# A hybrid encoder layer on one core: order of differences, tables, masks and late tiles up to attention, and splits, scales and places in the joints behind it

## The chip, the cores and the metric

The kernel is one program on one core of one Trainium2 chip. A core has engines that run side by side, each with its own queue of instructions that it works off in order: TensorE (PE) multiplies matrices into the accumulator memory PSUM, VectorE (DVE) does elementwise arithmetic, ScalarE (ACT) does activations, copies and casts, GpSimd (POOL) does odd elementwise work and issues transfers, SyncE (SP) only issues transfers. The metric is device microseconds (us) of one execution. The profile was taken on one execution of its own, and every row below is from it.

## The reference

One layer over 1024 tokens of width 1024, in float32. Three sub-layers follow each other, each between two RMS norms:

```python
h = swiglu(rmsnorm(x, ffn1_pre_g), ffn1_w_gate, ffn1_w_up, ffn1_w_down)   # 1024 -> 2816 -> 1024
x = x + 0.5 * rmsnorm(h, ffn1_post_g)
h = rmsnorm(x, mix_pre_g)
q, k, v = split(h @ w_qkv)                        # 16 heads of 64
o_na  = neighbourhood_attention(q[:8], k[:8], v[:8], na_rel_bias)      # 16 x 64 grid, window 8 x 16
o_dil = dilated_mixture_attention(q[8:], k[8:], v[8:], t5_rel_bias)    # windows (128,1), (512,4), (2048,16)
x = x + rmsnorm(concat(rmsnorm(o_na), rmsnorm(o_dil)) @ w_out, mix_post_g)
h = swiglu(rmsnorm(x, ffn2_pre_g), ffn2_w_gate, ffn2_w_up, ffn2_w_down)
x = x + 0.5 * rmsnorm(h, ffn2_post_g)
```

The matrix products of the two feed-forward layers, of q and k, of v and of the output projection carry nearly all of the work.

## The kernel before, in words

**Precision.** A float32 product is made of three faster ones (`mm3`, lines 317 to 319): each operand is split into a rounded part `hi` (a cast, on ACT, L413 or L673) and the rest `lo` (a subtraction, on DVE, L414 or L674), and hi*hi, hi*lo and lo*hi are summed in PSUM.

**Seven products for eight.** Each large product is cut into 2 x 2 blocks and done with seven block products on sums and differences of blocks (S1 to S4 on the left, T1 to T4 on the right). The tokens are 8 tiles of 128; tiles 0 to 3 are the upper half, 4 to 7 the lower. For a lower tile, the sums need the upper tile's block back: `early_half` loads it into a tile `x1` (a transfer issued by POOL, L212), and `right_half` makes the sums on DVE (L276 to L279, L272) and splits them (L268, L269).

**`PairGemm`** does gate and up (22 pairs) and q and k (8 pairs). The first `early` pairs run a part of their work `ahead` (the blocks A11 and A12, for which the lower tiles aren't needed yet), while the lower tiles are still being normed, transposed and summed. Then `run` goes over all pairs b; for an early pair it issues the products S2, the last product of the pair before (`last`), S1, S3 and S4 (12 matmuls each, `last` 12 too), 60 matmuls in all; a later pair does A11, `last`, S2, A12, S1, S3 and S4, 84 matmuls. Meanwhile it prepares the weights of pair b + 1: `direct` is three subtractions (L502 to L504) on weights just loaded, `second`, `sums` and `rest` are splits. On DVE there lie besides: u2 (L540), v (L548), c22 (L567), c21 (L575), and for q and k the `put` of each result: scale, cast (ACT, L925 to L930), subtraction (DVE, L931), and transfers to DRAM (POOL, L936 to L942). PE may begin S4 only when v has read the accumulator that S4 goes on with.

**`Passes`** does the down projections and v: seven passes over chunks, each chunk loaded (`praw`), cast (L673), subtracted (L674).

**The stages**, by the trace: first feed-forward layer with its early pairs, pair loop and seven down passes up to 690 us; early v passes and early q/k pairs to 768; the other v passes to 828; the pair loop of q and k to 946; attention (dilated heads, then neighbourhood heads) to 1184; output projection to 1265; second feed-forward layer, as the first, to the end at 1926.

**What sets the order.** PE runs in the order in which the program writes its instructions. For the other engines a planner sets the order, by its own estimates of durations: of the instructions whose inputs it takes to be ready, it puts an earlier written one first, and it may pull a later one ahead where it believes the engine idle. `c.behind(f, E)` takes that freedom away: what f issues on engine E stays behind the last instruction of E written so far. `plan(n, {turn: [...]})` hands out extra steps: one turn after each block of matmuls (`c.tick`). Steps with several parts go through `c.steps` and `c.sums`, from which every six matmuls take one each (`c.step`).

**Names used below.** `F` norms two tiles of the first layer, `A` adds the residual for two tiles and norms them (L788, then L150 on ACT, the small DVE steps L133 to L143, L204), `U` transposes a tile and makes its blocks (PE L157). `value_sums` are the differences of the v weights (`RightSums.sums`, DVE L385 to L387; one buffer `tr`, loaded again when the sums are stored). `masks` are nine steps of mask additions on POOL for the neighbourhood heads. `c.toeplitz` are eight transfers that spread the bias tables in DRAM (POOL, L852). `pg.start` loads the first two weight blocks, `split_left(0)` splits the first. `most` issues squares of the neighbourhood heads' outputs (ACT, L1213), whose norm (L131 to L143, L1220) the output projection needs first. `Finish.half` and `Finish.end` are the end of a layer: square on ACT (L150), product with the gain (DVE, L750), reciprocal root (L128 to L143), addition (L767), store (L768).

## Time and profile before

| | us |
|---|---|
| median of 3 runs | 1929.8 (1928.88 to 1931.73) |
| the profiled execution | 1927.83 |
| its span, first to last instruction | 1926.0 |
| PE busy | 1851.6 (96%) |
| DVE busy | 1325.9 (69%) |
| ACT busy | 832.0 (43%) |
| POOL busy | 319.9 (17%) |

A row of the timeline gives start, duration (both in us), engine, line of the kernel, operation, what it writes <- what it reads, the shape and how many in a row; in brackets the engine's idle time before it and what ended it. A row of the waits gives who waited for what: us in all, how many times, the longest. A row of the windows gives the stretch, its length, then for PE, PE's weight loads, DVE, ACT and POOL the busy us and the count of instructions, then the granted PE clock as a share of full speed, the share of time in which the transfer engines were busy, and GB/s.

### The profile page before, as it was taken

Reading aid. Unit: us, or ns where it says so; the run is one execution under the profiler, and the core shown is the slowest. Engines: PE = TensorE matmul, PEld = TensorE weight load, DVE = VectorE, ACT = ScalarE, POOL = GpSimd, SP = SyncE. Lnnn points to the kernel's source line nnn. Section 1 sums busy time; section 2 is a strip of 40 time slices with the busy share of each in tenths; the row PEclk is TensorE's granted clock in tenths of the full one; section 3 lists DMA queues with packets and bytes.
Section 4 is the critical chain, followed back from the end, with each engine's and each line's share of the span. In section 5 each row is a group of like instructions: output and inputs, shape, how many; then the busy total and the mean of one; then the engine's idle time right before and its main releaser. Section 6 shows DMA issues by size and latency. Waiting matters only on the chain.

```text
span 1926.0 us, 25147 instructions
## 1 busy us (share of the span) xinstructions
PE 1851.6 (96%) x8904; PEld 1536.5 (80%) x8904; DVE 1325.9 (69%) x2233; ACT 832.0 (43%) x1491; POOL 319.9 (17%) x504
## 2 busy tenths in 40 slices
PE   7899999999999989998899998999999999999997
PEld 6787888888778867877799997877888888888886
DVE  6777776765565875556677765777788777654557
ACT  7422333333344555223488765455222333344332
POOL 2123211111030122122433100121111111110000
PEclk9999999999999999999999999999999999999999
DMA  7656565547886757556968540575456655476563
GB/s 270 211 169 207 204 225 211 195 164 248 295 306 216 269 187 257 193 178 221 299 224 259 170 142 23 190 280 186 158 192 238 216 193 210 159 267 216 200 227 136
DMA packets 169296, 404.95 MB, mean 210 GB/s; under 512 B 17793, under 2 KB 40225, under 8 KB 167122
## 3 DMA queue, kind: packets, MB, share of 16 engines
q1 hardware_dynamic: 121330, 242.66, 37.9%
q0 software_dynamic: 46832, 158.59, 22.9%
q10 hardware_dynamic: 1008, 2.10, 0.3%
q8 instruction: 70, 1.15, 0.2%
q14 instruction: 56, 0.46, 0.1%
HBM read 277.34 MB, written 130.99 MB: 212 GB/s over the span
## 4 chain that ended last, share of the span: by engine, by line
PE 47%; issue 27%; DMA 9%; DVE 9%; POOL 3%; ACT 3%; SPq 1%; DVEq 0%; POOLq 0%; ACTq 0%
PE mmp L319 9%; PE mmp L317 9%; PE mmp L318 9%; PE accp L318 4%; PE accp L319 4%; PE accp L317 4%; PE po L1072 2%; PE ptp L982 2%; DMA wraw<-in_wqk_dram 2%; PE po L1184 2%; DMA wraw<-in_wu_dram 1%; DVE pw L674 1%; DMA tsv<-tr 1%; PE sp L1051 1%; DVE wlo L414 1%
## 5 line engine op out<-in xcount | busy, mean ns | idle before, releaser
L317 PE MATMUL mmp<-x,whi 128*128 128x512 f32 (+1 forms) x1464 | 581.4, 397 | 19.4 <-DVE v L548 10.9
L319 PE MATMUL mmp<-x,wlo 128*128 128x512 f32 (+1 forms) x1464 | 577.5, 394 | 3.9 <-DVE wlo L414 3.9
L318 PE MATMUL mmp<-x,whi 128*128 128x512 f32 (+1 forms) x1464 | 575.7, 393 | 1.3 <-DVE x L240 0.8
L317 PEld LDWEIGHTS mmp<-x,whi 128*128 128x128 f32 x1464 | 278.2, 190 | 84.7 <-ACT whi L413 10.0
L319 PEld LDWEIGHTS mmp<-x,wlo 128*128 128x128 f32 x1464 | 277.9, 190 | 68.6 <-DVE wlo L414 5.9
L318 PEld LDWEIGHTS mmp<-x,whi 128*128 128x128 f32 x1464 | 278.3, 190 | 62.6 <-DVE x L240 1.1
L674 DVE TENSOR_TENSOR pw<-praw,pw 128x1024 fp32r<-128x1024 f32 (+1 forms) x181 | 199.7, 1148 | 115.7 <-ACT pw L673 115.3
L673 ACT CAST pw<-praw 128x1024 fp32r<-128x1024 f32 (+1 forms) x181 | 168.6, 982 | 208.3 <-PE accp L319 150.3
L318 PE MATMUL accp<-pw 128*128 128x512 f32 x600 | 234.4, 391 | 5.9 <-DVE pw L674 5.6
L317 PE MATMUL accp<-pw 128*128 128x512 f32 x600 | 234.8, 391 | 0.3 <-DVE hb L730 0.2
L319 PE MATMUL accp<-pw 128*128 128x512 f32 x600 | 233.6, 389 | 0.0
L413 ACT CAST whi<-wraw 128x1024 fp32r<-128x1024 f32 x129 | 135.3, 1051 | 219.1 <-PE mmp L318 184.5
L414 DVE TENSOR_TENSOR wlo<-wraw,whi 128x1024 fp32r<-128x1024 f32 x129 | 158.2, 1228 | 19.9 <-ACT whi L413 19.7
L318 PEld LDWEIGHTS accp<-pw 128*128 128x128 f32 x600 | 112.7, 188 | 31.6 <-DVE pw L674 9.0
L317 PEld LDWEIGHTS accp<-pw 128*128 128x128 f32 x600 | 112.7, 188 | 25.1 <-ACT pw L673 1.2
L319 PEld LDWEIGHTS accp<-pw 128*128 128x128 f32 x600 | 112.6, 188 | 23.3
L621 POOL DMA_DIRECT2D g<-sg x44 | 23.9, 544 | 471.1 <-DVE sg L614 296.4
L413 ACT CAST whi<-traw 128x512 fp32r<-128x512 f32 x52 | 32.4, 623 | 152.3 <-DVE traw L503 95.6
L502 DVE TENSOR_TENSOR wraw<-wraw 128x1024 f32<-128x1024 f32 x52 | 63.7, 1225 | 45.4 <-DMA wraw<-in_wqk_dram 26.2
L432 ACT COPY s<-mmp 128x512 f32<-128x512 f32 x52 | 30.6, 588 | 139.4 <-PE mmp L319 136.4
L575 DVE TENSOR_TENSOR c<-mmp,u 128x512 f32<-128x512 f32 x52 | 35.9, 690 | 76.9 <-PE mmp L319 76.8
L1184 PE MATMUL po<-vs,pt 128*128 128x128 f32 x352 | 50.3, 276 | 2.0 <-ACT pt L984 1.7
(278 smaller groups left out, 2761.1 us busy)
## 6 DMA issues: line engine op xcount, KB each, us to landing
praw<-g SPq DMA_DIRECT2D x70, 512.0 KB, 6.0
wraw<-in_wg_dram SPq DMA_DIRECT2D x44, 512.0 KB, 4.2
wraw<-in_wu_dram SPq DMA_DIRECT2D x44, 512.0 KB, 6.2
tr<-in_wd_dram SPq DMA_DIRECT2D x44, 512.0 KB, 6.5
g<-sg POOLq DMA_DIRECT2D x88, 256.0 KB, 4.1
ts<-tr POOLq DMA_DIRECT2D x22, 1024.0 KB, 4.8
praw<-ts SPq DMA_DIRECT2D x88, 256.0 KB, 4.3
praw<-in_wd_dram SPq DMA_DIRECT2D x66, 256.0 KB, 4.9
```

The lines of the kernel that those rows point to most:

```text
L317: nc.tensor.matmul(out, ahi, bhi, start=start, stop=False, skip_group_check=go_on)
L318: nc.tensor.matmul(out, ahi, blo, start=False, stop=False, skip_group_check=go_on)
L319: nc.tensor.matmul(out, alo, bhi, start=False, stop=stop, skip_group_check=go_on)
L413: nc.scalar.copy(hi, raw)
L414: nc.vector.tensor_sub(lo, raw, hi.bitcast(F32))
L502: nc.vector.tensor_sub(r[:, 0:2], r[:, 1:3], r[:, 0:2])
L575: nc.vector.tensor_add(c21, d, u2)
L673: nc.scalar.copy(hi, raw[:, :m])
L674: nc.vector.tensor_sub(lo, raw[:, :m], hi.bitcast(F32))
L982: nc.tensor.transpose(ps[:, j, :], src[:, j * P:(j + 1) * P], c.ident)
L1072: nc.tensor.matmul(po[:, un * 2 + j], pt[:, 2 * j + t, :], rhs, start=t == 0, stop=t == 1)
L1184: nc.tensor.matmul(po[0][:, u], pt[0][:, j, :], vs[:, k0 + j, :], start=j == 0, stop=j == n - 1)
```

## The change

Nothing is computed otherwise; instructions change place, order, queue or buffer.

- **Differences.** `direct` of the pair loop (three subtractions on DVE) is pinned behind the last DVE instruction written before it.
- **Tiles.** In the first layer, the norm of tiles 6 and 7 is written one turn earlier and both norms are pinned on ACT; the transposes of tiles 6 and 7 come one turn later. For q, k, v the transposes of tiles 4 to 7 come later and the residual of tiles 6, 7 is written at turn 10 instead of 4. In the second layer tiles 6 and 7 come one turn earlier. Outside the first layer the upper half for tiles 5 and 7 is loaded into a buffer of the `x` tiles, as soon as tile 4 or 5 has been transposed, and that of tile 6 when tile 4 is done.
- **Masks and tables.** The mask steps alternate with the differences of the v weights, two to one; the eight table transfers go from the pair loop of q and k to the v passes before it, one every second turn.
- **q and k.** The second half of k is put away right after its sum (`third`) and no longer with the second half of q in `last`; the last pair's q goes to DRAM by SP instead of POOL.
- **Joints.** `most` is called one turn earlier and takes a turn at once. In the second layer the first weights are loaded two turns earlier, and their split is made before the layer begins, into a buffer of its own. In the last layer the product with the gain goes into a tile `hm` of its own for the first half of tiles 4 to 7.

```diff
         self.parts[t] = deque(((A11, xn[:, :T]), (A12, xn[:, T:])))
-        if t >= 4:
+        if t == 4 or t > 4 and c.xn:
             self.early_half(t)
     def early_half(self, t):
         c = self.c
-        x1 = self.half[t] = c.xp.tile([P, 2, 4, P], F32, tag="x1", name="x1", bufs=c.deep)
+        if t % 2 and not c.xn:
+            x1 = c.xp.tile([P, D], F32, tag="x", name="x1", bufs=c.xbufs).rearrange("p (i k x) -> p i k x", i=2, k=4)
+        else:
+            x1 = c.xp.tile([P, 2, 4, P], F32, tag="x1", name="x1", bufs=c.deep)
+        self.half[t] = x1
...
             self.open -= 1
+            if t == 4 and not c.xn:
+                self.early_half(6)
         a22 = transposed(c, src)
+        if t in (4, 5) and not c.xn:
+            self.early_half(2 * t - 3)
...
                 if last:
                     last()
-                direct()
+                c.behind(direct, DVE)
                 second()
...
                 self.sink.first(b, pb, False, s1)
-                direct()
+                c.behind(direct, DVE)
                 second()
...
             nc.vector.tensor_add(c22, d, v)
+            self.sink.third(b, c22)
             sums()
...
         sumsq(self.c, h, self.ss[:, t, g:g + 1])
-        self.c.nc.vector.tensor_mul(h, h, self.gain[:, g * T:(g + 1) * T])
+        to = h
+        if self.last and t >= 4 and g == 0:
+            to = self.part = self.c.xp.tile([P, T], F32, tag="hm", name="hm")
+        self.c.nc.vector.tensor_mul(to, h, self.gain[:, g * T:(g + 1) * T])
...
-            nc.vector.scalar_tensor_tensor(x[:, sl], h[:, sl], r, x[:, sl], op0=ALU.mult, op1=ALU.add)
+            nc.vector.scalar_tensor_tensor(x[:, sl], h[:, sl] if g else self.part, r, x[:, sl], op0=ALU.mult, op1=ALU.add)
...
+    def third(self, b, k):
+        self.put(b, 1, 1, k)
+
     def last(self, b, q, k):
         self.put(b, 0, 1, q)
-        self.put(b, 1, 1, k)
...
-                nc.gpsimd.dma_start(dst, e[:, j].bitcast(F32).rearrange("p (s x) -> p s x", s=8))
+                (nc.sync if h and b == 7 else nc.gpsimd).dma_start(dst, e[:, j].bitcast(F32).rearrange("p (s x) -> p s x", s=8))
...
-            early_pools(e)
+            early_pools(e, 2 if pg.own else 3)
...
-            spread(more + masks, 36)
+            steps = more[:1]
+            for i, f in enumerate(more[1:]):
+                steps += masks[2 * i:2 * i + 2] + [f]
+            spread(steps + masks[2 * len(more[1:]):], 36)
...
-            F = lambda *ts: lambda: op0.norm(ts, [xs[t] for t in ts])
+            F = lambda *ts: lambda: c.behind(lambda: op0.norm(ts, [xs[t] for t in ts]), ACT)
...
-                                    {0: [F(4, 5), L(6, 7)], 1: [U(4)], 2: [F(6, 7), U(5)], 4: [U(6)], 5: [U(7)]},
+                                    {0: [F(4, 5), L(6, 7)], 1: [U(4), F(6, 7)], 2: [U(5)], 5: [U(6)], 6: [U(7)]},
...
-            plan(12, {0: [lambda: fin.scale(4, 4), A(4, 5)], 4: [A(6, 7)], 7: [U(4)], 9: [U(5), lambda: queued(pg.start)],
-                      11: [lambda: pg.split_left(0)]})
+            plan(12, {0: [lambda: fin.scale(4, 4), A(4, 5)], 8: [U(4), lambda: queued(pg.start)],
+                      10: [lambda: pg.split_left(0), A(6, 7)]})
             vp.run(0, 1, upto=1)
...
-            plan(8, {1: [U(6)], 3: [U(7)]})
+            plan(8, {0: [U(5)], 3: [U(6)], 5: [U(7)]})
             pg.ahead()
...
+            plan(20, {2 * i: [f] for i, f in enumerate(c.toeplitz)})
             vp.run(2, 3)
...
-            plan(8, {**{i: c.toeplitz[2 * i:2 * i + 2] for i in range(4)}, 5: [lambda: queued(load_head)], 7: [lambda: queued(load_head), lambda: queued(first_bias),
+            plan(8, {5: [lambda: queued(load_head)], 7: [lambda: queued(load_head), lambda: queued(first_bias),
...
                     c.todo.append(lambda n=n, i=i: c.behind(lambda: n.squares(slice(0, 448), 0, (i, i + 1)), ACT))
+            c.tick()
...
-                        c.todo.extend([lambda: None, most])
+                        c.todo.append(most)
...
+            pg.own = pool("p0", 1, prep, side="right")
...
-            plan(12, {0: [lambda: fin.scale(0, 4), A(0, 1)], 2: [A(2, 3)], 5: [U(0)], 6: [U(1)], 7: [G(4)],
-                      8: [lambda: queued(pg.start), G(5)], 9: [U(2)], 10: [U(3)], 11: [G(6)]})
+            plan(12, {0: [lambda: fin.scale(0, 4), A(0, 1)], 2: [A(2, 3)], 5: [U(0)], 6: [U(1), lambda: queued(pg.start)], 7: [G(4)],
+                      8: [G(5)], 9: [U(2)], 10: [U(3), lambda: pg.split_left(0)], 11: [G(6)]})
...
-                {0: [G(7), lambda: fin.scale(4, 4), A(4, 5)], 1: [A(6, 7)], 3: [U(4)], 4: [U(5)], 6: [U(6)], 7: [U(7)]},
+                {0: [G(7), lambda: fin.scale(4, 4), A(4, 5)], 1: [A(6, 7)], 3: [U(4)], 4: [U(5)], 5: [U(6)], 6: [U(7)]},
```

More of the change, by code (lines that the diff above doesn't have):

```diff
@@ L622, in second, with third @@
         self.got[b, 0] = g
+    def third(self, b, up):
+        pass
     def last(self, b, gate, up):
@@ L739, with __init__ @@
 class Finish:
-    def __init__(self, c, src, dst, gain, op):
-        self.c, self.src, self.dst, self.gain, self.op = c, src, dst, gain, op
+    def __init__(self, c, src, dst, gain, op, last=False):
+        self.c, self.src, self.dst, self.gain, self.op, self.last = c, src, dst, gain, op, last
         self.ss = c.small.tile([P, 8, 2], F32, tag="fss", name="fss", bufs=1)
@@ L1373, in ffn @@
             c.pw, c.pr, c.ha, c.tj = pool("pw", 5, w), pool("pr", 4, w), pool("ha", 1, w), pool("tj", 1, m)
-            fin = Finish(c, src, dst, load_gain(c, post, "post"), None)
+            fin = Finish(c, src, dst, load_gain(c, post, "post"), None, pre is None)
             hs = {}
```

## The prediction

> **What bounds the kernel now.** I read the page first, then the waits of PE, then windows around each of these waits, then the timeline inside them.
>
> ```profile
> PE 1851.6 (96%) x8904; PEld 1536.5 (80%) x8904; DVE 1325.9 (69%) x2233; ACT 832.0 (43%) x1491; POOL 319.9 (17%) x504
> ```
>
> PE is busy for 1851.6 of 1926.0 us, so an edit that leaves its work alone can win at most what PE stands still or runs slowly for. The waits of PE (total, times, longest) say where:
>
> ```profile
> PE mmp L317 <- DVE v L548: 10.9, 7, 2.8
> PE accp L318 <- DVE pw L674: 6.0, 7, 1.7
> PE trp L157 <- DVE x L204: 5.5, 1, 5.5
> PE trp L157 <- DVE xn L204: 4.9, 1, 4.9
> PE gps L304 <- DMA xn<-in_ffn_pre_g_dram: 4.4, 1, 4.4
> PE mmp L317 <- ACT whi L413: 4.4, 2, 2.3
> PE mmp L319 <- DVE wlo L414: 3.9, 3, 3.1
> PE po L1072 <- ACT pt L984: 3.2, 4, 1.0
> PE sp L1051 <- DVE sa L972: 2.9, 1, 2.9
> PE mmp L317 <- ACT x L238: 2.6, 1, 2.6
> PE trp L1231 <- DVE og L1220: 2.5, 1, 2.5
> ```
>
> Of these only L304 (the kernel's start) and L1072 (inside attention) lie where nothing is changed. Windows of the places that the change touches (length, then busy time, granted clock, DMA share, GB/s):
>
> ```profile
> 26.00:35.00 9.00, 5.55 (x19) 4.01 (x18) 5.05 (x16) 4.25 (x9) 3.75 (x7) 0.81 1.02 406
> 40.00:62.00 22.00, 16.47 (x72) 12.94 (x72) 18.66 (x36) 13.65 (x23) 4.09 (x8) 0.92 0.70 234
> 480.00:545.00 65.00, 59.00 (x249) 45.82 (x248) 37.31 (x40) 28.67 (x39) 4.67 (x7) 1.00 0.86 302
> 695.00:728.00 33.00, 24.38 (x100) 19.25 (x99) 26.13 (x52) 19.09 (x33) 10.09 (x18) 0.90 0.63 214
> 775.00:860.00 85.00, 83.45 (x366) 68.16 (x364) 52.10 (x66) 22.78 (x26) 16.75 (x28) 1.00 0.51 167
> 855.00:882.00 27.00, 21.79 (x90) 17.30 (x89) 18.72 (x24) 9.99 (x12) 9.36 (x14) 0.94 0.72 207
> 882.00:945.00 63.00, 57.55 (x251) 46.46 (x250) 39.53 (x53) 19.82 (x28) 15.86 (x22) 1.00 0.82 270
> 945.00:960.00 15.00, 10.31 (x58) 9.42 (x56) 7.66 (x29) 10.26 (x28) 9.15 (x9) 0.77 1.00 340
> 1184.00:1204.00 20.00, 15.61 (x75) 11.72 (x74) 15.20 (x50) 7.78 (x28) 0.60 (x2) 0.91 0.00 1
> 1264.00:1274.00 10.00, 7.50 (x22) 5.32 (x21) 8.70 (x20) 4.46 (x9) 1.63 (x4) 0.66 0.76 263
> 1305.00:1340.00 35.00, 31.37 (x133) 23.96 (x132) 27.56 (x40) 20.13 (x34) 6.48 (x12) 0.95 0.56 189
> 1340.00:1690.00 350.00, 350.00 (x1526) 286.18 (x1525) 261.44 (x331) 105.76 (x140) 46.73 (x82) 1.00 0.56 194
> 1915.00:1926.00 11.00, 0.57 (x3) 0.14 (x1) 6.60 (x21) 0.72 (x2) 0.00 (x0) 0.67 0.26 95
> ```
>
> The pair loop from 1340 to 1690 shows PE full: 350/1526 = 0.229 us a matmul, so a turn of 12 is 2.75 us and one of 24 is 5.5. In the other windows the loss has two parts: the idle time (length less PE's busy time) and the slow clock (length times one less the granted clock).
>
> **The change part by part.** Each place with its loss, what I take of it and, in brackets, both ends.
>
> (1) *Norm of tiles 4 and 5 pinned on ACT.* Loss in 26–35: 3.45 + 9 x 0.19 = 1.7.
>
> ```profile
> 27.64 1.07 ACT L150 ACTIVATE xn<-x 128x1024 f32<-128x1024 f32 x1
> ```
>
> This square was pulled ahead of the cast L238 that PE waits 2.6 for. Pinned, it comes after; but the same norm then ends about two squares (2.1) later, and ACT's queue holds back L413 while a tile is still being loaded. Take 1.5 [-1: the 2.6 gone and two squares and a split of 1.5 in exchange; 4].
>
> (2) *Tiles 6, 7: norm a turn earlier, transposes a turn later.* Loss in 40–62: 5.53 + 1.76.
>
> ```profile
> 56.58 2.48 DVE L204 SCALAR_TENSOR_TENSOR xn<-x,y,gain 128x1024 f32<-128x1024 f32 x2
> ```
>
> PE waits 4.9 for it, with 18.66 of 22 us of DVE taken by sums and splits. The norm starts up to a turn (5.5) earlier and PE asks a turn later: more than the wait. What may be late next is tile 7's splits ahead of the pair loop, now 5.5 nearer to it. Take 6 [3: half the wait and its clock; 7.3].
>
> (3) *Differences of the v weights between the masks.* Loss in 480–545: 6.0, for L674.
>
> ```profile
> 516.00 1.23 DVE L385 TENSOR_TENSOR tr<-tr 128x1024 f32<-128x1024 f32 x1 [7.35 <-DMA tr<-in_wv_dram]
> ```
>
> With one buffer `tr`, each group is stored before the next load; DVE waits in order, and L674 behind it. With two masks between, the steps are six to eight turns apart (16 to 22 us) and the load has landed. What covers it: the transfers, already at 0.86 of their time here, with the mask additions now in the same stretch on POOL, where the stores queue behind them. Take 4.5 [0; 6].
>
> (4) *Residual of tiles 4 to 7 for q, k, v.* Loss in 695–728: 8.62 + 3.3.
>
> ```profile
> 692.42 4.87 DVE L788 SCALAR_TENSOR_TENSOR x<-hb,y,x 128x1024 f32<-128x1024 f32 x4
> ```
>
> Two of these four (1.22 each) and a second reciprocal root leave from ahead of L204, for which PE waits 5.5, and U(4) comes 2.75 later: 2.4 + 2.75 = 5.2 of the 5.5. The other wait, 3.1 for L414, stood behind tile 5's sums, which move to `ahead`; but there the residual and norm of tiles 6, 7 now take DVE for two L788 (2.4), two L204 (2.48 by the row in (2)) and some ten small steps (1.7), 6.6 together, so I count half. With the clock, take 7.5 [3: the wait of 3.1 alone; 11.9].
>
> (5) *`direct` pinned in q and k; tables and k put elsewhere.* Loss in 855–882 and 882–945: 5.21 + 5.45, clock 1.6.
>
> ```profile
> 870.08 1.23 DVE L502 TENSOR_TENSOR wraw<-wraw 128x1024 f32<-128x1024 f32 x1 [6.64 <-DMA wraw<-in_wqk_dram]
> ```
> ```profile
> 877.08 0.68 DVE L548 TENSOR_TENSOR v<-mmp,u 128x512 f32<-128x512 f32 x1
> ```
>
> L502 was pulled ahead and holds DVE for 6.64 until weights land; behind it stand L906, L540, and L548, for which PE waits 10.9 in seven pairs. Pinned behind q's `put`, it starts some 9 us into the pair, after the landing, and v is no longer behind it. Eight table transfers leave POOL here (15.86 of 63 us busy) for the v passes, where transfers stand at 0.51 and POOL at 16.75 of 85 us: cost 0 there, at worst one L674 wait of 1.7. Putting k earlier moves a cast, a subtraction and two transfers past L906 and `sums`: no count changes. Take 10.5 [4: if only the 6.64 pair mends; 12.3].
>
> (6) *Last pair's k put early, its q by SP.* Loss in 945–960: 4.69 + 3.45.
>
> ```profile
> 951.42 2.13 POOL L961 CAST q<-st 128x1024 fp32r<-128x1024 f32 x1
> ```
>
> A subtraction of k leaves from ahead of L972 (PE waits 2.9) and two transfers from ahead of this cast. SP issues them instead, with the loads of `va` queued behind: these are read a head later. The 1.00 of the transfers in this window keeps most. Take 2.5 [0; 5].
>
> (7) *`most` two ticks earlier.* Loss in 1184–1204: 4.39 + 1.8.
>
> ```profile
> 1184.44 0.15 DVE L131 TENSOR_TENSOR v<-gss 128x4 f32<-128x4 f32 x1
> ```
>
> The squares behind it come some 3 us sooner, more than the 2.5 that PE waits for L1220. The last head's own result comes when it comes. Take 5 [2; 6.2].
>
> (8) *First split of the second layer before it starts.* Loss in 1264–1274: 2.5 + 3.4; L413 of the first weights is the wait of 2.3. Two casts leave; pair 1's split must then fit into 12 matmuls. Take 5 [2; 5.9].
>
> (9) *`x1` buffers and turns in the second layer.* Loss in 1305–1340: 3.63 + 1.75.
>
> ```profile
> 1307.90 0.69 DVE L278 TENSOR_TENSOR s<-s,x 128x512 f32<-128x512 f32 x1 [2.82 <-DMA x<-xn]
> ```
>
> The upper half is loaded before it is asked for; tiles 6 and 7 follow a turn (5.5) earlier, for which DVE, at 27.56 of 35, has room. Take 4.5 [0; 5.4].
>
> (10) *The tile `hm`.* PE is done at 1915.57 by the window.
>
> ```profile
> 1917.50 0.69 DVE L733 TENSOR_TENSOR hb<-accp,hb 128x512 f32<-128x512 f32 x1
> 1919.03 0.69 DVE L750 TENSOR_TENSOR hb<-hb,gain 128x512 f32<-128x512 f32 x1 [0.85 <-ACT junk L150]
> ```
>
> L733 runs 1.9 late because DVE's chain a tile is longer than PE's. L750 no longer waits 0.85 for ACT's read of the same tile, in each of the last four. Take 2.6: 0.7 at the last and the 1.9 [0.7; 3].
>
> *The charge: `direct` pinned in the feed-forward layers*, where nothing was lost.
>
> ```profile
> 112.92 0.69 DVE L540 TENSOR_TENSOR u<-mmp,s 128x512 f32<-128x512 f32 x1
> ```
> ```profile
> 121.00 0.69 DVE L638 TENSOR_TENSOR sg<-sg 128x512 f32<-128x512 f32 x1
> ```
> ```profile
> L413 ACT CAST whi<-traw 128x512 fp32r<-128x512 f32 x52 | 32.4, 623 | 152.3 <-DVE traw L503 95.6
> ```
>
> L540 reads the first product of a pair; 12 matmuls and the read-out of 0.4 before it, at 109.8, the pair began. An early pair has 60 matmuls (13.8 us), so PE asks for the next T2 at 123.6. If the pair before was odd, `last` ends with L638. L502 (1.23), L503 (0.68 as L548), the cast (0.62) and L414 (0.68) from 121.7 on end at 124.9, of which about 0.9 shows. Four such pairs a layer: 8 x 0.9 = 7 [0: DVE has slack; 8 x 2.8, the longest wait for v, = 22]. The other pairs have `last` done by the middle, or 84 matmuls.
>
> Sum: 1.5 + 6 + 4.5 + 7.5 + 10.5 + 2.5 + 5 + 5 + 4.5 + 2.6 = 49.6, less 7 is 42.6. The profiled execution took 1927.8 in all (1.8 around its span), so 1885; the median of the runs is 2.0 above it, so 1887.
>
> A rule against four of these terms: the Trainium skill ("TensorE: Matmul & The Clock Gate", part 1, the HAM clock gate) says that the clock halves only after a whole idle window of about 3.4 us. The windows at 26, 1184 and 1264 show 0.81, 0.91 and 0.66 with no listed wait there above 2.6, so in this trace shorter waits sufficed, or the cause is another.
>
> **The rivals.**
> - *The pins cost everywhere (slower).* 22 + 22 + 8 pairs: if the split of T2 came late in each, the change loses from 49.6/52 = 0.95 us a pair on; at 1.5 it is 78 - 49.6 = 28 slower, 1958. For: DVE is busy 261 of 350 us. Against: that leaves a quarter free, and a later pair has 19 us for `last`, `direct` and the split.
> - *The planner pulls other work ahead.* Turns moved without a pin do nothing; (5), (7), (8), (9), (10) hold: 27.6 - 7 = 20.6, 1909. For: the squares of (1), written later, ran first. Against: in (4) what leaves is ahead by program order.
> - *Transfers stay the limit in (3) and (5):* 15 less, 1902. For: shares of 0.82 and 0.86. Against: L502 waits for one load, not for all.
> - *The slow clock stays though the waits go:* 1.7 + 1.6 + 1.8 + 3.4 + 1.75 = 10.3 less, 1897. For: dips at short waits. Against: 1.00 wherever PE is fed.
>
> **How the numbers follow.** The forecast 0.55, the pins 0.07, the planner 0.16, the transfers 0.12, the clock 0.08, no change 0.02. A measurement here tells about 0.2% (4 us), so faster 0.91, same 0.02, slower 0.07. The likeliest's own range is 1872 (15 of the 17 by which the upper ends, 67 in all, exceed the takes) to 1897; with the transfers, the clock and the planner in, 1872 to 1910.
>
> **What would show it.** Right: the rows of L548, of both L204, of L385's and L502's waits for transfers gone or below 1; the windows at (1), (8) with clock above 0.9; L733 less than 0.5 after PE's last. Wrong: new waits of mmp for `whi` or `wlo` made from `traw` (the charge), of L674 around 775–860, or of L157 for L204 a turn later than now. What would upset the forecast is a pinned `direct` behind something that itself waits, as in (5), only elsewhere.

## The result and the profile after

The changed kernel takes 1915.2 us in the median (1914.1 to 1916.5) beside 1930.8 for the kernel before: a ratio of 0.9938, with an interval of 0.9921 to 0.9955. It is faster, by 12 us (0.6%), where 43 were forecast, and it lies 5 above the range. The profiled execution has a span of 1913.4 against 1926.0.

Line numbers moved: L413 and L414 (split of a weight) are now L421 and L422, L385 (v weights' differences) L393, L502 to L504 (`direct`) L510 to L512, L548 (v) L556, L567 (c22) L575, L673 and L674 L685 and L686, L852 (tables) L867, L931 L948.

The page of the changed kernel, the line of the engines:

```profile
PE 1846.7 (97%) x8904; PEld 1532.9 (80%) x8904; DVE 1331.3 (70%) x2233; ACT 830.7 (43%) x1491; POOL 318.7 (17%) x502
```

The waits of PE in the changed kernel (us in all, times, longest):

```profile
PE mmp L327 <- DVE wlo L422: 10.9, 9, 2.6
PE mmp L325 <- ACT whi L421: 7.5, 6, 2.2
PE accp L325 <- ACT pw L685: 5.0, 4, 3.2
PE accp L326 <- DVE pw L686: 4.6, 7, 0.9
PE gps L312 <- DMA xn<-in_ffn_pre_g_dram: 4.4, 1, 4.4
PE sp L1068 <- DVE sa L989: 3.5, 1, 3.5
PE po L1089 <- ACT pt L1001: 3.4, 5, 1.0
PE trp L157 <- DVE xn L204: 3.1, 1, 3.1
```

The 10.9 for v (L556 now) are gone, and so are the long waits for tile 6's L204 and for L204 ahead of q, k, v. At the head of the list stand two that were small before: splits of weights (3.9 and 4.4 before). Windows of the changed kernel (columns as before) show where they are:

```profile
26.00:42.00 16.00, 11.40 (x55) 8.39 (x53) 11.47 (x25) 11.61 (x20) 4.29 (x8) 1.00 0.98 369
40.00:62.00 22.00, 21.66 (x103) 17.39 (x102) 20.29 (x39) 15.56 (x27) 5.42 (x10) 1.00 0.71 241
74.00:86.00 12.00, 9.20 (x32) 6.74 (x32) 5.09 (x7) 3.60 (x5) 1.16 (x3) 0.86 0.70 237
118.00:128.00 10.00, 7.89 (x34) 5.86 (x33) 8.13 (x11) 1.66 (x2) 3.76 (x7) 1.00 0.72 243
480.00:545.00 65.00, 61.72 (x265) 48.93 (x263) 37.84 (x37) 29.44 (x40) 15.76 (x21) 1.00 0.94 330
690.00:728.00 38.00, 35.69 (x161) 28.30 (x160) 32.80 (x70) 23.61 (x39) 13.03 (x23) 1.00 0.80 265
775.00:792.00 17.00, 11.98 (x48) 9.05 (x47) 9.98 (x13) 4.61 (x5) 0.00 (x0) 0.92 0.71 240
824.00:933.00 109.00, 109.00 (x482) 90.34 (x481) 81.45 (x105) 41.26 (x52) 28.54 (x40) 1.00 0.70 225
...
1345.00:1450.00 105.00, 96.28 (x408) 76.84 (x407) 80.37 (x108) 21.73 (x27) 14.61 (x27) 0.98 0.51 168
```

Tile 6's window is full now (21.66 of 22), and so is the whole pair loop of q and k (109 of 109). New idle time stands at 74–86, at 118–128, in the v passes (5.0 of 17 at 775–792) and at the start of the second feed-forward loop (8.7 of 105). Two of the prediction's signs of being wrong have come up: waits for `whi` and `wlo` in the early pairs, and waits for chunks in the v passes. The lengths of the stages in the two traces, each from the start of its first product to the next stage's, give the balance (us). The two loops begin with their early work (`ahead`), and what lies between the dilated heads and the last heads, the same in both traces, is left out:

| stage | before | after | difference | terms of the prediction |
|---|---|---|---|---|
| first feed-forward loop | 451.4 | 455.7 | +4.3 | (1), (2), half the charge: -1.5 - 6 + 3.5 |
| its down passes, first v passes | 254.0 | 245.1 | -8.9 | (3) and a part of (4) |
| `ahead` of q and k | 51.1 | 47.1 | -4.0 | the rest of (4); together 12 |
| v passes | 55.4 | 64.7 | +9.3 | tables: 0 |
| pair loop of q and k | 122.5 | 108.8 | -13.7 | (5): -10.5 |
| dilated heads | 172.6 | 170.6 | -2.0 | (6): -2.5 |
| last heads, output projection | 87.0 | 81.6 | -5.4 | (7), (8): -10 |
| second feed-forward loop | 438.4 | 447.7 | +9.3 | (9), half the charge: -4.5 + 3.5 |
| its down passes | 209.8 | 210.2 | +0.4 | |
| behind PE's last matmul | 10.5 | 8.4 | -2.0 | (10): -2.6 |

### The profile page after: what moved, and what is told of

The parts are those of the page before. It is cut to its first block, busy times and chain, and to the rows that moved or that the text cites. A ratio compares the mean times of both kernels' runs of the same rounds, so it can differ in the third digit from the quotient of the medians.

```text
span 1913.4 us, 25103 instructions
## 1 busy us (share of the span) xinstructions
PE 1846.7 (97%) x8904; PEld 1532.9 (80%) x8904; DVE 1331.3 (70%) x2233; ACT 830.7 (43%) x1491; POOL 318.7 (17%) x502
## 4 chain that ended last, share of the span: by engine, by line
PE 64%; issue 16%; DVE 7%; DMA 6%; ACT 4%; POOL 2%; SPq 0%; DVEq 0%; POOLq 0%; ACTq 0%
PE mmp L327 11%; PE mmp L326 10%; PE mmp L325 10%; PE accp L326 8%; PE accp L327 8%; PE accp L325 8%; PE po L1089 2%; PE ptp L999 2%; PE po L1201 2%; DVE wlo L422 1%; PE sp L1068 1%; PE trp L157 1%; ACT whi L421 1%; PE sp L1185 1%; DVE pw L686 1%
## 5 line engine op out<-in xcount | busy, mean ns | idle before, releaser
L327 PE MATMUL mmp<-x,wlo 128*128 128x512 f32 (+1 forms) x1464 | 576.9, 394 | 10.9 <-DVE wlo L422 10.9
L686 DVE TENSOR_TENSOR pw<-praw,pw 128x1024 fp32r<-128x1024 f32 (+1 forms) x181 | 201.6, 1158 | 128.8 <-ACT pw L685 128.5
L421 ACT CAST whi<-wraw 128x1024 fp32r<-128x1024 f32 x129 | 135.2, 1050 | 320.1 <-PE mmp L326 246.9
L685 ACT CAST pw<-praw 128x1024 fp32r<-128x1024 f32 (+1 forms) x181 | 168.9, 981 | 205.8 <-PE accp L327 144.6
L422 DVE TENSOR_TENSOR wlo<-wraw,whi 128x1024 fp32r<-128x1024 f32 x129 | 157.8, 1224 | 23.4 <-ACT whi L421 23.0
L421 ACT CAST whi<-traw 128x512 fp32r<-128x512 f32 x52 | 32.3, 621 | 98.9 <-DVE traw L511 98.7
L510 DVE TENSOR_TENSOR wraw<-wraw 128x1024 f32<-128x1024 f32 x52 | 63.5, 1221 | 7.8 <-DMA wraw<-in_wqk_dram 7.0
```

Source lines behind the costliest of these rows:

```text
L327: nc.tensor.matmul(out, alo, bhi, start=False, stop=stop, skip_group_check=go_on)
L421: nc.scalar.copy(hi, raw)
L422: nc.vector.tensor_sub(lo, raw, hi.bitcast(F32))
L510: nc.vector.tensor_sub(r[:, 0:2], r[:, 1:3], r[:, 0:2])
L685: nc.scalar.copy(hi, raw[:, :m])
L686: nc.vector.tensor_sub(lo, raw[:, :m], hi.bitcast(F32))
```

## The experiments

Each was timed beside the kernel before on the same chip; ratios are to that. "The loop" of a layer is its stage in the table above; idle time is a stage's length less PE's busy time in it. One trace gives a stage to a few us only: in eleven traces in which the first loop is the same (new order, no pin there) it took 447.0 to 451.9, in eleven in which the second is the same (new turns, no pin there) 435.9 to 437.7. The idle times in them, 7.4 to 8.2 and 5.9 to 6.3, repeat better; the granted clock differs (1.00 in the first loop of 447.0, 0.98 in that of 451.9).

The theory to begin with (A): the pin of `direct` in the feed-forward layers was sized too small, and the tables cost in the v passes. The rival (B): the shortfall lies in the joints.

### The pin undone in the feed-forward layers

```diff
-                c.behind(direct, DVE)
+                c.behind(direct, DVE) if isinstance(self.sink, QKPairs) else direct()
```

> The changed kernel with direct pinned for q and k alone; in the two feed-forward layers it is placed by the planner again. Theory A (the pin in the feed-forward layers is the term that was too small: the waits of mmp for whi and wlo in their early pairs come to about 20 us in the trace of the changed kernel, 2 before): 18 to 20 less than the changed kernel, 1895 to 1898, and the waits for L421 and L422 there gone. Theory B (the shortfall lies in the joints, and the early pairs would wait for something else without the pin): less than 6 gained, 1909 to 1915.

Measured: 1898.8, ratio 0.9852 (0.9831 to 0.9872), 16.6 less than the changed kernel by the ratios. The loops went from 455.7 to 448.3 and from 447.7 to 437.5, together 17.6. Theory A. DVE's timeline in the changed kernel shows why a pair costs more than 0.9:

```profile
118.75 0.69 DVE L650 TENSOR_TENSOR sg<-sg 128x512 f32<-128x512 f32 x1
119.36 1.22 DVE L510 TENSOR_TENSOR wraw<-wraw 128x1024 f32<-128x1024 f32 x1
120.49 0.68 DVE L575 TENSOR_TENSOR c<-mmp,v 128x512 f32<-128x512 f32 x1
121.09 0.68 DVE L511 TENSOR_TENSOR traw<-wraw 128x512 f32<-128x512 f32 x1
121.81 1.22 DVE L422 TENSOR_TENSOR wlo<-wraw,whi 128x1024 fp32r<-128x1024 f32 x1
122.95 0.68 DVE L512 TENSOR_TENSOR wraw<-wraw,traw 128x512 f32<-128x512 f32 x1
123.56 0.68 DVE L422 TENSOR_TENSOR wlo<-traw,whi 128x512 fp32r<-128x512 f32 x1
```

`direct` starts behind `last` (L650), as forecast. But before the last split that T2 needs (the L422 of `traw`), three more get in: c22 (L575), the split of the other weight (L422 on `wraw`) and L512: 2.6 us by these rows. The split and L512 read what L510 writes, so the pin made them late with T2's chain. c22 waits for PE's S3, pin or no pin. The kernel before shows c22 and that split at just this place, behind `last` (L638 at 121.00), while its L502 had run at 109.38:

```profile
121.61 0.68 DVE L567 TENSOR_TENSOR c<-mmp,v 128x512 f32<-128x512 f32 x1
122.21 1.22 DVE L414 TENSOR_TENSOR wlo<-wraw,whi 128x1024 fp32r<-128x1024 f32 x1
```

PE stood first for `whi`, then for `wlo`. By its timeline this comes in seven pairs, three in the first loop and four in the second: 1.1 us of waits in two of them, 2.1 to 2.4 in the other five, 13.0 together. Without the pin the idle time of the two loops is 12.3 less (12.6 to 7.6, 13.3 to 6.0); the rest of the 17.6 is that the same matmuls ran slower.

### The same pin alone, on the kernel before

```diff
-                direct()
+                c.behind(direct, DVE) if not isinstance(self.sink, QKPairs) else direct()
```

> The kernel before with one edit: direct pinned in the two feed-forward layers. Theory A (the pin alone makes the weights of the early pairs late, whatever else is changed): waits of mmp for whi and wlo of 15 to 19 in those pairs, 1943 to 1946. Theory B (the pin costs only with the moved tiles and the split made early): within 5 of the kernel before.

Measured: 1947.7, ratio 1.0112 (1.0092 to 1.0132). The loops are 460.1 and 447.8, 18.1 more than before. The waits of PE in the second one, from 1340 to 1480:

```profile
PE mmp L319 <- DVE wlo L414: 4.5, 4, 1.2
PE mmp L317 <- ACT whi L413: 4.2, 4, 1.1
```

The same seven pairs stall. So the pin costs this by itself, without the other edits. The planner's freedom to run L502 as soon as the weights are there was worth 18 us.

### The pin, the tables and the loop of q and k

On the kernel before, the pin for q and k alone:

```diff
-                direct()
+                c.behind(direct, DVE) if isinstance(self.sink, QKPairs) else direct()
```

> The kernel before with one edit: direct pinned for q and k. Theory A (the pin alone takes away the waits for v): about 11 less than the kernel before, 1919. Theory B (it needs the tables and the second half of k out of the way as well): 3 to 6 less, 1925 to 1927.

Measured: 1932.4, ratio 1.0023 (1.0007 to 1.0039). Neither expectation holds: no gain, and a loop of 126.4 against 122.5. The waits in the loop, from 840 to 950, have changed their name:

```profile
PE mmp L317 <- ACT whi L413: 8.3, 3, 2.9
PE mmp L317 <- DVE v L548: 1.2, 2, 0.7
PE mmp L319 <- DVE wlo L414: 1.1, 3, 0.7
```

v hardly waits behind L502 any more, but L502, pinned behind the `put`s of q and k, is itself too late. So I asked the other way round, the changed kernel with no pin at all:

```diff
-                c.behind(direct, DVE)
+                direct()
```

> The changed kernel with direct pinned nowhere. Theory A (the pin, the earlier half of k and the moved tables are needed together for q and k): the waits of mmp for v come back in the pair loop of q and k, some 8 to 11, so 1906 to 1910 against 1898 with the pin for q and k alone. Theory B (the moved tables and the earlier half of k alone mend the pair loop): 1896 to 1900, no waits for v there.

Measured: 1899.1, ratio 0.9863 (0.9847 to 0.988). The loop of q and k is 108.8, just as with the pin, and PE waits for v nowhere in it. Theory B: the pin did nothing there. Then the tables back into the loop, first with the pins of the changed kernel:

```diff
-            plan(20, {2 * i: [f] for i, f in enumerate(c.toeplitz)})
...
-            plan(8, {5: [lambda: queued(load_head)], 7: [...
+            plan(8, {**{i: c.toeplitz[2 * i:2 * i + 2] for i in range(4)}, 5: [lambda: queued(load_head)], 7: [...
```

> The changed kernel with the eight table transfers back in the pair loop of q and k. Theory A (they crowd the loads of the v passes; PE waits about 5 there for chunks that land late): 4 to 6 less than the changed kernel, 1909 to 1911, with the waits of accp for L685 and L686 around 785 gone and no waits for v in the pair loop, since direct is pinned there. Theory B (the loads are late for another reason, or the tables cost in the pair loop what they cost here): within 2 of the changed kernel.

Measured: 1918.3, ratio 0.9948 (0.993 to 0.9966). Neither: the v passes went from 64.7 to 57.1 as A has it, but the loop of q and k from 108.8 to 120.7, with 5.8 of waits for `whi` and `wlo`. The same edit with no pin anywhere:

> The changed kernel with direct pinned nowhere and the table transfers back in the pair loop of q and k; the earlier half of k stays. Theory A (the transfers of the tables were what made the weights late there, and so the waits for v): waits of mmp for v of some 8 to 11 in the pair loop come back, none in the v passes, 1901 to 1904. Theory B (the earlier half of k mended the pair loop): no waits for v, 5 less than with the tables in the v passes, 1893 to 1895.

Measured: 1906.8, ratio 0.9899 (0.9884 to 0.9914); loop 124.4, v passes 57.5. Theory A, though 3 above its range: the waits for v are back.

```profile
PE mmp L325 <- DVE v L556: 11.0, 6, 4.9
```

And DVE's timeline shows the old picture, weights that land late and hold the queue:

```profile
857.84 1.23 DVE L510 TENSOR_TENSOR wraw<-wraw 128x1024 f32<-128x1024 f32 x1 [8.00 <-DMA wraw<-in_wqk_dram]
```

The loop of q and k, in us, with k's second half put early:

| | tables in the loop | tables in the v passes |
|---|---|---|
| `direct` pinned | 120.7 (117.5 in the run below) | 108.8 |
| not pinned | 124.4 | 108.8 |

The 13.7 won in that loop come with the tables' leaving. Their transfers delayed the weights: the loads of `wraw` took up to 10.9 us to land in that loop before (median 7.1), up to 5.9 (median 4.8) in the changed kernel, and up to 12.0 with the tables back and no pin. The pin eased that by 4 to 7 where the tables stayed and k was put early; with k late it cost 3.9 (126.4 against 122.5); where the tables had gone it did nothing. The early k gained nothing by itself (124.4 against 122.5). No run has the tables gone and k late, so whether both are needed is open.

Pins undone in the feed-forward layers and tables back, together:

> Both of the edits before together. If the two causes are separate places, their gains add up: 1890 to 1893. If the one only hides the other, no better than the first alone (1895 to 1898).

Measured: 1898.1, ratio 0.9852 (0.9834 to 0.9871): no better than the first alone. v passes 56.2, loop of q and k 117.5; what the passes gave back, the loop took. For the whole kernel the tables' new place is worth nothing with the pin in q and k alone, 0.1% with all pins (0.9948 to 0.9938, within the intervals) and 0.4% with none (0.9899 to 0.9863).

### A later place for the tables

In the v passes of the changed kernel POOL issues the first four tables in one piece, since its queue stood behind q's and k's stores when their turns came:

```profile
763.58 0.89 POOL L957 DMA_DIRECT2D qk<-qk  x1 [0.44 <-DVE qk L948]
764.46 2.36 POOL L867 DMA_DIRECT2D gab<-tab  x4
```

Twenty us later PE waits 3.2 for a chunk: the loads of chunks took up to 12.2 us to land here, 5.7 with the tables back in the loop. With the pin for q and k, and the tables later:

```diff
-            plan(20, {2 * i: [f] for i, f in enumerate(c.toeplitz)})
+            plan(20, {8 + i: [f] for i, f in enumerate(c.toeplitz)})
```

> The kernel with direct pinned for q and k alone, and the table transfers one a turn from turn 8 of the v passes on instead of every second turn from turn 0. Theory A (four of them leave in one burst at 756 to 759, ahead of the loads of the pass after, and these land late): the waits of accp of 3.1 and 1.2 around 776 to 781 go, 4 less, 1894 to 1895, and no whi wait comes in the pair loop. Theory B (the loads are late by the weights of the first pairs, which leave at the same time): no change, 1898.

Measured: 1901.1, ratio 0.9872 (0.9857 to 0.9887). The v passes are 57.0 and the chunks land within 6.2, so A is right that the early tables delayed them. That it is their leaving in one burst is not shown: later and spread are one edit here, and the next run issues four at once too, at 791.9. But one wait of 9.6 stands in the loop of q and k. ACT's timeline there:

```profile
853.48 1.09 ACT L947 CAST qk<-c 128x512 fp32r<-128x512 f32 x1 [9.82 <-DMA qk<-qk]
854.47 1.04 ACT L421 CAST whi<-wraw 128x1024 fp32r<-128x1024 f32 x1
```

The casts of an earlier `put` had ended by 842.5, but DVE ran their subtractions (L948) only from 848.4 on, behind a sum that waited for PE, and POOL issued the stores at 850.6. So the cast L947 waited for the buffer, and the next L948, L511 behind it and the split of `traw` were late in turn. Would it cost as much if `direct` were not pinned behind the subtractions of those `put`s?

> The changed kernel with direct pinned nowhere and the table transfers one a turn from turn 8 of the v passes on. Theory A (the wait of 9.6 for whi at 847 came because direct was pinned behind a subtraction L948 that the planner had put late): without the pin that wait is gone and the waits of accp of 3.0 and 2.1 at 776 to 780 are gone too, 5 to 7 less than with direct pinned nowhere and the tables from turn 0, 1892 to 1894. Theory B (late tables make the loads of q and k's weights late whoever waits): a wait of 5 or more in the first pairs remains, 1899 to 1902.

Measured, with no pin and late tables: 1894.7, ratio 0.9836 (0.9815 to 0.9858). The 9.6 are gone (the longest wait of L947 for a store is 1.6); v passes 59.0, loop of q and k 111.5, with 2.2 of waits for v. Theory A for the pin; the 5.9 of the passes are gained and 2.7 of them given back in the loop. By the medians this is 4 better than the tables from turn 0; the intervals overlap.

### The first layer's tiles, the masks, the joint before q and k

These three start from the kernel with the pin for q and k alone (1898.8, 0.9852). First the transposes of tiles 4 and 5 a turn later, for the new wait of 3.1 for L204:

```diff
-{0: [F(4, 5), L(6, 7)], 1: [U(4), F(6, 7)], 2: [U(5)], 5: [U(6)], 6: [U(7)]}
+{0: [F(4, 5), L(6, 7)], 1: [F(6, 7)], 2: [U(4)], 3: [U(5)], 5: [U(6)], 6: [U(7)]}
```

> The kernel with direct pinned for q and k alone, and in the first layer the transposes of tiles 4 and 5 a turn (24 matmuls, 5.5 us) later. Theory A (pinning the norm on ACT made L204 of tile 4 late by 3.3 where PE asks for it): this wait goes and nothing comes in its place, 3 less, 1895. Theory B (the lower tiles are then late for the pair loop, where whi is waited for at 79 already): the wait moves, 1898 to 1901.

Measured: 1897.6, ratio 0.9852 (0.9838 to 0.9867). Theory B by the waits: the one for L204 fell to 0.9, and two of 2.4 and 2.2 for `wlo` came at 54 and 71; the loop is 449.1 against 448.3, its idle time 7.5 against 7.6. Norm and turns all as before:

```diff
-F = lambda *ts: lambda: c.behind(lambda: op0.norm(ts, [xs[t] for t in ts]), ACT)
+F = lambda *ts: lambda: op0.norm(ts, [xs[t] for t in ts])
-... 1: [U(4), F(6, 7)], 2: [U(5)], 5: [U(6)], 6: [U(7)]}
+... 1: [U(4)], 2: [F(6, 7), U(5)], 4: [U(6)], 5: [U(7)]}
```

> The kernel with direct pinned for q and k alone, and norm and transposes of the first layer's tiles 4 to 7 as in the kernel before. By the gaps of PE the new order took 5.7 from tile 6's L204 and gave back 1.2 at tile 4, so 4 to 5 more than with it, 1902 to 1903; if the slow clock follows the waits, 5 to 6. If the order is worth nothing, 1898.

Measured: 1901.5, ratio 0.9871 (0.9856 to 0.9886), 3.7 more by the ratios and by the loop (452.0). By these (1) and (2) are worth 3.7 together, where 7.5 were taken, and even that is not clear of noise: the ratios' intervals overlap, and the idle time is only 1.7 more (9.3 against 7.6; 9.7 in the kernel before). Tile 6's wait went, and in exchange came the 3.1 for tile 4 and, at the end of `ahead`, 2.2 for `whi` at 78. The masks:

```diff
-            steps = more[:1]
-            for i, f in enumerate(more[1:]):
-                steps += masks[2 * i:2 * i + 2] + [f]
-            spread(steps + masks[2 * len(more[1:]):], 36)
+            spread(more + masks, 36)
```

> The kernel with direct pinned for q and k alone, and the differences of the v weights all ahead of the masks, as in the kernel before. By the gaps of PE from 480 to 545 the alternation took 3 to 5: 3 to 5 more than with it, 1901 to 1903, and L385's line waits up to 7 for its load again. If the masks in that stretch cost what the differences gain: 1898.

Measured: 1902.5, ratio 0.9878 (0.9865 to 0.9892), 5.0 more; the down passes (with the first v passes) are 250.6 against 244.2, and L393 waits up to 7.6 for its load again, where the alternation left 1.3. The term (3), 4.5, holds. The joint:

```diff
-... 8: [U(4), lambda: queued(pg.start)], 10: [lambda: pg.split_left(0), A(6, 7)]})
+... 4: [A(6, 7)], 7: [U(4)], 9: [U(5), lambda: queued(pg.start)], 11: [lambda: pg.split_left(0)]})
-            plan(8, {0: [U(5)], 3: [U(6)], 5: [U(7)]})
+            plan(8, {1: [U(6)], 3: [U(7)]})
```

> The kernel with direct pinned for q and k alone, and the residual and transposes of tiles 4 to 7 for q, k, v as in the kernel before. By the gaps of PE the waits of 5.5 and 3.1 went and some 4 new ones for chunks of the v passes came: 5 more than with it, 1903, 8 more with the slow clock. If the upper halves' earlier load did it and not the order of turns: the wait for wlo stays away and only the 5.5 comes back, 1903 too, so the list of waits decides.

Measured: 1901.4, ratio 0.9868 (0.9851 to 0.9885), 3.1 more; the two stages come to 297.8 against 291.3, 6.5 more. The wait for L204 is back (6.3), the one for `wlo` is not (0.4 is left of 3.1). So of (4) the turns mended the first wait; the second went without them, so most likely by the buffers and early loads of the upper halves, which stayed.

### The later joints, the tail, and a better version

These start from the version with no pin and late tables (1894.7, 0.9836). Four joints as before:

```diff
-            c.tick()
-                        c.todo.append(most)
+                        c.todo.extend([lambda: None, most])
-            pg.own = pool("p0", 1, prep, side="right")
-... 6: [U(1), lambda: queued(pg.start)], ... 8: [G(5)], ... 10: [U(3), lambda: pg.split_left(0)] ...
+... 6: [U(1)], ... 8: [lambda: queued(pg.start), G(5)], ... 10: [U(3)] ...
-... 5: [U(6)], 6: [U(7)]}
+... 6: [U(6)], 7: [U(7)]}
```

> The version with direct pinned nowhere and late tables, with four of the later joints as in the kernel before: most's two ticks, the first split of the second feed-forward layer and its buffer, and the turns of its tiles 6 and 7. The forecast took 14.5 for these with the x1 buffers, which stay; the gaps of PE in the changed kernel say 7. Theory A (the gaps): 1900 to 1902. Theory B (the forecast's takes, with the slow clock): 1906 to 1909.

Measured: 1894.8, ratio 0.984 (0.9825 to 0.9855). Neither: they are worth nothing together. The traces say why: last heads and projection took 3.8 more (86.8 against 83.0), the second feed-forward loop 5.4 less (430.9 against 436.3), with 1.1 of idle time against 6.3. One of the edits loses there:

```diff
-... 5: [U(6)], 6: [U(7)]}
+... 6: [U(6)], 7: [U(7)]}
```

> The version with direct pinned nowhere and late tables, and in the second feed-forward layer the turns of tiles 6 and 7 as in the kernel before; most and the first split keep their new places. Theory A (the stage from the layer's first product to its down passes took 436.3 with the new turns and 430.9 with four joints undone, so the earlier turns lose 5.4 there): 5 less, 1889 to 1890, with the waits of L157 for L273 between 1266 and 1285 gone. Theory B (the early split, not the turns, made that stage longer): 1894 to 1895.

Measured: 1891.9, ratio 0.9816 (0.98 to 0.9833); the loop is 433.0, 3.3 less, with 3.3 of idle time, and the projection keeps its 81.6. That lies between the theories, and the ratios' intervals overlap; the loop is clear of the 435.9 to 437.7 with the new turns. The waits of PE from 1238 to 1310 in the version with the new turns begin so:

```profile
PE trp L157 <- DVE x L273: 3.1, 3, 1.8
PE mmp L325 <- ACT whi L421: 1.5, 1, 1.5
```

With the old turns no wait of L157 is left there. A turn earlier, PE asks for the transposes before DVE has split the tile ahead of them.

This run and the one before it differ only by (7) and (8), and show where (8) went. Up to the loop the new places win 5.2: the wait for L1237 (L1220 before) fell from 2.4 to 0.7, and those for the first split, 2.3 and 0.7, gave way to one of 1.4 for L238. In the loop 2.1 are lost again: waits for `whi` of 1.2 and 1.5 and for `wlo` of 0.5 stand where one of 0.4 stood. Splitting the first weight early moved the wait to the weights behind it.

The same question in the first layer, on top of that:

```diff
-... 5: [U(6)], 6: [U(7)]},
+... 4: [U(6)], 5: [U(7)]},
```

> As the run before this, and in the first layer the transposes of tiles 6 and 7 a turn earlier, as in the kernel before, with the norm kept a turn early: L204 of tile 6 ends at 53 and PE asked at 52.8 in the kernel before. Theory A (the waits of 2.2 and 0.6 for whi and wlo around 80 come from tile 7's late splits): 2 to 3 less than the run before this, 1886 to 1888. Theory B (they come from the weights' split at the loop's start): no change, and up to 1 for L204.

Measured: 1888.6, ratio 0.9806 (0.9793 to 0.982). The first loop went from 449.3 to 445.1, the waits around 80 from one of 2.2 to one of 1.2. Theory A in direction; the gain between the two runs is within their intervals. This version beats both kernels: 25 less than the changed one by the ratios.

Last, the tail without `hm`:

```diff
-        if self.last and t >= 4 and g == 0:
+        if False:
...
+            nc.vector.scalar_tensor_tensor(x[:, sl], h[:, sl], r, x[:, sl], op0=ALU.mult, op1=ALU.add)
```

> The version with direct pinned nowhere and late tables, without the tile hm. By the trace the stretch behind PE's last matmul is 8.4 with hm and 10.5 without, so 2 more, 1896 to 1897, with L750 waiting for ACT again. If the tail is set by the transfers out: no change.

Measured: 1896.2, ratio 0.9859 (0.9835 to 0.9883), too close to tell by time; behind PE's last matmul lie 10.8 us in its trace against 8.4 with `hm`. The 2 us of (10) hold by the trace.

## Why the prediction was wrong

The direction was right, and the time was not. Three steps failed.

- **The charge, "8 x 0.9 = 7".** The mechanism was right, the size was not: 17.6 undone, 18.1 alone. Seven pairs stalled, not eight, at some 2.5 each. The step "L502, L503, the cast and L414 from 121.7 on" counted T2's own chain and took DVE for free behind it. But c22 and the other weight's split (1.9 us) stood at that very place in the trace before (121.61 and 122.21), and L512 comes with the chain: 2.6 in all that queue into it. The forecast took a value near the lower end of 0 to 22; what was measured lies near the upper.
- **(5), cause and price of the tables.** "Pinned behind q's `put` ... v is no longer behind it" gave the gain to the pin, and the tables "cost 0 there, at worst one L674 wait of 1.7". The gain (13.7) is there with and without the pin and goes with the tables; that it came out above the 10.5 taken was luck, since the step named for it did not do it. The v passes took 9.3 more, 7.6 of which go when the tables do (64.7 to 57.1). The transfers' 0.51 over 85 us hid this: the tables leave just ahead of loads of the passes, with the transfers at 1.05 from 760 to 775. The pin by itself, on the kernel before, only renamed the wait.
- **(1), (2), (7), (8), (9): takes near the upper end.** 22 were taken. (1) and (2) gave 3.1 of 7.5 by the stages (451.4 to 448.3 without the pin), since stalls came at the next tile and at the loop's start. (7) and (8) gave 5.4 of 10 in their stage, of which 2.1 came back in the loop behind it, where the weights after the first split were then late. (9) gave 0.9 of 4.5 (438.4 to 437.5): with its turns and the first split as before that loop took 430.9, so the buffers won more than was taken, and the turns (3.3) and the early split (2.1) gave most of it back. In (1), (2) and (8) the prediction had named what would be late next, and priced it at little or nothing; in (9) it held that DVE, at 27.56 of 35, had room.

(3), (4), (6) and (10) hold in size: 12.9 for the 12 of (3) and (4) by the stages, 2.0 for 2.5, 2.0 for 2.6. In (4) the second wait did not go by the step named. (6) has no run of its own, and its stage took 170.6 to 172.1 in the versions that keep it. The sum by the table: 42.6 less 10.6 (charge), 9.3 (tables), 4.4 (first layer's tiles), 4.6 (joints), 3.6 (second layer's tiles), 1.1 (6 and 10), plus 3.2 (more won in the loop of q and k) and 0.9 (3 and 4), leaves 13.1 against 12.6 measured.

Of the rivals, "the pins cost everywhere" had the right culprit and the wrong number of pairs: of 52 seven stalled, and its 1.5 a pair was less than the 2.5 that each cost. "Transfers stay the limit in (5)" was near too: what bounded that loop was a transfer, and the pin could not mend it.

## What to carry to other kernels

A pin on a queue costs more than its own chain: what comes ready at the same moment queues into it. Count each instruction that queues between the pinned one and the one that is waited for. When a wait goes through an engine's queue to a transfer, look for what crowds the transfer before the order of the queue; move that work, and price its new place too (here 5.9 to 7.6 were lost in the v passes for 8.7 to 15.6 won in the loop). And for a step moved a turn earlier or later, give the stall that takes its place a price, since in both feed-forward layers more than half of the gain that was forecast did not come.

## What the runs showed of the hardware

The length of a stall did not tell whether the clock fell. In the changed kernel a stall of 3.1 at 32.7 left the clock at 1.00, one of 3.2 at 785.3 was followed by 0.57 and 0.50, and a shorter one, 2.2 at 77.8, by 0.83 and 0.73; windows of the stalls and of what follows:

```profile
32.70:36.20 3.50, 0.42 (x3) 0.07 (x2) 3.33 (x8) 1.81 (x2) 1.07 (x2) 1.00 1.03 346
36.20:40.00 3.80, 3.80 (x22) 3.17 (x23) 2.53 (x4) 2.75 (x5) 0.00 (x0) 1.00 1.03 409
785.30:788.90 3.60, 0.37 (x2) 0.00 (x0) 3.60 (x6) 2.04 (x3) 0.00 (x0) 1.00 0.07 27
788.90:792.00 3.10, 2.15 (x5) 1.55 (x6) 3.10 (x4) 0.90 (x1) 0.00 (x0) 0.57 0.40 122
792.00:796.00 4.00, 4.00 (x10) 3.10 (x10) 0.72 (x2) 0.00 (x0) 1.17 (x2) 0.50 0.99 359
...
77.80:80.40 2.60, 0.41 (x3) 0.05 (x1) 0.58 (x1) 2.14 (x4) 0.54 (x1) 1.00 0.81 304
80.40:84.00 3.60, 2.99 (x10) 2.08 (x11) 2.38 (x3) 0.85 (x1) 0.00 (x0) 0.83 0.31 126
84.00:88.00 4.00, 4.00 (x14) 3.17 (x13) 2.45 (x3) 0.00 (x0) 0.00 (x0) 0.73 0.96 298
```

The Trainium skill ("TensorE: Matmul & The Clock Gate", part 1, the HAM clock gate) says that the watching window runs freely, which agrees with nearly equal stalls that end differently; that it takes a whole idle window of about 3.4 us does not agree with the stall of 2.2 at 77.8 here.
